# Fixed TensorE order in the experts, with weight buffers of 4 and 8 KB

## The chip, the cores and the metric

The kernel runs on one core of a Trainium2 chip, as one launch. The metric is the device time in microseconds; the kernel before was run three times. The profiler took one further execution of it, from which all rows below come. A core has five engines that each work through their own instructions in order: PE (matrix products), DVE, ACT and POOL (elementwise work and copies) and SP (which here only starts transfers). 16 DMA engines move data between the chip's memory and the core's own memory, SBUF, which has 128 partitions.

## The reference

One layer of a streaming encoder over 512 tokens of width 1024, in f32: a mixing block (pooling mixer and sparse attention), cross-attention into 256 memory tokens, and a mixture of experts. The last of these is what the change is about. A router takes the best of 4 groups and, in it, the best 2 of 8 experts for each token; each of the 32 experts has three matrices of 1 MB:

```python
h = rmsnorm(x, g)                       # (512, 1024)
for g in range(4):                      # groups of 8 experts
    a = einsum('nd,edf->nef', h, w_gate[g])     # 1024 -> 256
    b = einsum('nd,edf->nef', h, w_up[g])       # 1024 -> 256
    hid = silu(a) * b * gates[:, g, :, None]
    out += einsum('nef,efd->nd', hid, w_down[g])  # 256 -> 1024
x = x + out
```

## The kernel before

The layer before the experts works in four tiles of 128 tokens. After the cross-attention, `ffn_in(t)` (L1085 on) takes tile t of the residual x: PE transposes it, ACT and DVE copy the transposes (L1104, L1109), ACT sums the squares (L1105) and starts two transfers of the rows, to `hd`, a table in memory (L1106), and to the output `out` (L1107). Router products (L1115), `route` (L971 on: DVE finds groups and experts) and `seats` (place of a token in its expert) follow. `select` makes a 0/1 matrix from tokens to seats.

Each expert has 64 seats. The experts go in 16 pairs, and the two of a pair use the two column halves of PE. For pair i the kernel does this, all in f32:

- `slot_rows` and `slot_factors` (L1040, L1048), for two pairs at a time: PE multiplies the 0/1 matrix by small columns (L1034), which gives the row index of each seat (`idx`) and its two factors (`gc`).
- `fetch` (L1059): POOL starts a gather of the 128 rows from `hd` by `idx`, into one of three buffers. `buffer` (L1016) sets such a buffer to zero on POOL when it is first used.
- `turn_rows` (L1072): 8 transposes of 128x128 on PE into one tile of PSUM (`sc`), scaled by DVE to `xt`.
- `experts` (L1203): 32 matmuls of gate, 32 of up; each takes 64 seats by 128 rows of the weight's 1024 (chunk c of 8, for both experts k in turn). SiLU on ACT (L1208), product on DVE (L1213).
- `rest`: two transposes of the hidden values (L1219), 16 matmuls of down (L1230), copies of y by ACT and DVE (L1232, L1233), and a scatter by POOL (L1235) that adds the rows of y to `out` by `idx`.

What sets the order: the program is written once, and a scheduler (the Tile framework) then orders each engine's instructions and puts in the waits. Buffers for everything large are kept by `Slots`: 42 buffers of 4 KB per partition, and 8 more when an earlier pool is closed. `Stream` loads weights ahead through them, in the order of their use: whenever a buffer is put back, `pump` starts the next load as long as a reserve of free buffers stays (the numbers r1 to r7). The buffer that a load gets is fixed when the program is built, first freed, first used, and the load waits at run time for the last reader of that buffer. A matrix of an expert is loaded in two halves of 512 KB, 128 partitions by 4 KB; `do_load` (L249) starts them all on SP. The 96 matrices make 192 loads.

Transfers that SP and ACT start share eight completion semaphores in turn, so each waits for the one eight places before it.

Of the kernel before, what the change touches and what calls it, by code (L numbers as in the profile page):

```python
# [36 lines left out]
NSLOT = 42  # L37
NSLOT2 = 8
NG_BUF = 3
# [9 lines left out]
           t0=44, tp=1.75, a0=128, ap=1.6, d1=1, d2=2, r1=10, r2=10, r3=4, r4=11, r5=3, raw=3, raw2=4, mm=4,  # L49
# [11 lines left out]
class Slots:  # L61


    def __init__(self, pool, n):
        self.pools, self.free, self.n, self.where = {}, [], 0, {}
        self.on_put = lambda: None
        self.more(pool, n)

    def more(self, pool, n):
        self.pools.update({s: pool for s in range(len(self.pools), len(self.pools) + n)})  # L70
        self.free += list(self.pools)[-n:]

    def get(self, shape, dt):
        s = self.free.pop(0)
        self.n += 1
        t = self.pools[s].tile(shape, dt, tag=f"s{s}", name=f"s{s}_{self.n}")
        self.where[id(t)] = (s, t)
        return t

    def take_out(self):  # L80
        return self.free.pop(0)

    def again(self, s, shape, dt):
        self.n += 1
        return self.pools[s].tile(shape, dt, tag=f"s{s}", name=f"s{s}_{self.n}")

    def put(self, *tiles):
        for t in tiles:
            self.free.append(self.where.pop(id(t))[0])
        self.on_put()  # L90


class Stream:
# [28 lines left out]
    def pump(self, need=None):  # L122
# [3 lines left out]
        while True:  # L126
# [4 lines left out]
            elif (self.n_load < len(self.items) and len(self.S.free) >= 1 + keep  # L131
# [60 lines left out]
def kernel(ctx, tc, A, out, dbg=None):  # L192
# [10 lines left out]
    S = Slots(slot_pool, NSLOT)  # L203
# [42 lines left out]

    def do_load(src, shape):
        raw = S.get(shape, F32)
        sp.dma_start(raw, src)  # L249
        return raw  # L250

    def do_split(raw, gain, eng):
        shape = list(raw.shape)
        hi, lo = S.get(shape, F32R), S.get(shape, F32R)
# [233 lines left out]
    def evac_k(t, ps):  # L488
# [10 lines left out]
        if t % 2 == 0:  # L499
            kT[t // 2] = [S.get([P, 2, 4, P], F32R) for _ in range(2)]  # L500
# [96 lines left out]
    def load_bands():  # L597
        pw["b"] = [S.get([P, 1024], F32R) for _ in range(2)]
# [140 lines left out]
    def memory():  # L739
# [9 lines left out]
        kmT.extend(S.get([P, MH, MT], F32R) for _ in range(2))  # L749
# [77 lines left out]
    def transposed(t):  # L827

        hl = [S.get([P, NC, P], F32R) for _ in range(2)]
# [124 lines left out]
    row = keep.tile([P, NT, 2], F32R, name="row")  # L954
    row_f = keep.tile([P, NT, 2], F32, name="row_f")
    inf = keep.tile([P, NT, NPR, 4], F32R, name="inf")
# [3 lines left out]
    pool.tensor_copy(row, row_f)  # L960
# [69 lines left out]
    def per_slot(sel, i, cols_of, n):  # L1030

        pi = tr_tile([P, 512])
        for t in range(NT):
            pe.matmul(pi[:, :n], sel[:, t, cols(i)], cols_of(t), start=(t == 0), stop=(t == NT - 1))  # L1034
        return pi[:, :n]

    def slot_rows(j):
        for i in range(2):
            idx = fin.tile([P, 1], I32, tag="idx", name="idx", bufs=6)
            dve.tensor_scalar(idx, per_slot(sels[j], i, lambda t: row[:, t], 2)[:, 0:1], float(OOB), None, op0=OP.add)  # L1040
            tabs_[2 * j + i] = [idx, None]

    def slot_factors(j):
        sel = sels.pop(j)
        for i in range(2):
            gc = fin.tile([P, 2], F32, tag="gc", name="gc", bufs=6)
            pi = per_slot(sel, i, lambda t: inf[:, t, 2 * j + i], 4)
            dve.tensor_reduce(gc, pi.rearrange("p (a b) -> p a b", b=2), axis=AX.X, op=OP.add)  # L1048
            tabs_[2 * j + i][1] = gc

    def fetch(i):

        if i >= NPR:
            return
        if i % 2 == 0 and i not in tabs_:
# [302 lines left out]
```

## Time and profile before

| | us |
|---|---|
| median of 3 runs | 618.62 |
| lowest, highest | 615.48, 623.16 |
| the profiled execution | 623.07 |
| its span | 621.2 |
| PE busy in the span | 558.6 (90%) |
| DVE, ACT, POOL busy | 312.9, 191.7, 115.1 |

The span runs from the first to the last instruction of the profiled execution; its time is the device's, and has some 2 us around the span. The mean clock granted to PE in it is 0.944 of full speed. The first 340 us are the layer up to the router, in which weights are loaded ahead; the experts' matmuls run from 365 to 606 us. In the rows, a number of a stretch is from the start of the span. "out<-in" gives the tile written and the tile read by the program's names, "xN" the count, and a bracket the idle time of the engine ahead of the row and what ended it.

### The profile page before, as it was taken

The page shows a single profiled execution, that of the slowest core. Times are in us where ns is not written, and L with a number is a line of the kernel's source. Part 1 is how long each engine was busy: PE and PEld are TensorE (multiplying, and loading weights), DVE is VectorE, ACT ScalarE, POOL GpSimd, SP SyncE. Part 2 cuts the span into 40 slices and gives each one's busy share as a digit, 9 for nine tenths or more (in the row PEclk, how much of TensorE's full clock was granted, in tenths as well). Part 3 has the DMA queues.
Part 4 walks back from the last instruction along what each step waited for, and adds up shares of the span by engine and source line. Part 5 has one row for each costly group of instructions (what it writes and reads, how often), then busy time and mean ns, then how long its engine had stood idle before and what let it go on. Part 6 is the DMA issues. An engine that isn't in the chain of part 4 may idle for free.

```text
span 621.2 us, 9049 instructions
## 1 busy us (share of the span) xinstructions
PE 558.6 (90%) x3408; PEld 395.8 (64%) x3408; DVE 312.9 (50%) x752; ACT 191.7 (31%) x366; POOL 115.1 (19%) x94
## 2 busy tenths in 40 slices
PE   8997989999979999999989589979898979899880
PEld 4776766887767777788878466555555555555430
DVE  4598999998996656544435723222222222022000
ACT  5573534424555567764432110101010100001000
POOL 0323331201363000030001211121212121211111
PEclk9998999999989999999989759979897989899996
DMA  8963021326661201129999849999999999999962
GB/s 291 379 207 103 1 69 68 121 82 190 217 216 41 79 0 35 32 79 324 336 338 365 309 135 344 396 397 391 399 382 386 357 383 360 390 355 372 339 222 32
DMA packets 52833, 147.86 MB, mean 238 GB/s; under 512 B 10288, under 2 KB 11056, under 8 KB 52784
## 3 DMA queue, kind: packets, MB, share of 16 engines
q1 hardware_dynamic: 47024, 134.62, 59.6%
q0 software_dynamic: 4608, 8.40, 5.6%
q10 hardware_dynamic: 1152, 4.19, 1.7%
q8 instruction: 29, 0.48, 0.3%
q14 instruction: 20, 0.16, 0.1%
HBM read 142.99 MB, written 12.58 MB: 250 GB/s over the span
## 4 chain that ended last, share of the span: by engine, by line
PE 65%; DMA 15%; DVE 9%; issue 4%; ACT 3%; POOL 2%; SPq 0%; POOLq 0%; DVEq 0%; ACTq 0%
PE mm L1203 15%; PE mm L342 9%; PE mm L343 9%; PE mm L344 8%; PE mm L1230 8%; DMA out_dram<-s,idx 6%; DMA s<-in_w_up_dram 2%; PE sc L352 2%; PE sc L1072 2%; DMA s<-in_w_down_dram 2%; DMA s<-in_w_in_dram 2%; PE tr L1034 2%; PE tr L919 1%; PE tr L698 1%; PE tr L711 1%
## 5 line engine op out<-in xcount | busy, mean ns | idle before, releaser
L1203 PE MATMUL mm<-s,s 128*64 128x256 f32 x1024 | 135.9, 409 | 5.5 <-ACT sg L1208 3.5
L342 PE MATMUL mm<-s,s 128*128 128x512 f32 (+1 forms) x320 | 132.5, 417 | 0.9 <-ACT s L257 0.7
L343 PE MATMUL mm<-s,s 128*128 128x512 f32 (+1 forms) x320 | 127.6, 399 | 1.2 <-DVE s L259 0.8
L344 PE MATMUL mm<-s,s 128*128 128x512 f32 (+1 forms) x320 | 127.6, 399 | 0.0
L1203 PEld LDWEIGHTS mm<-s,s 128*64 128x64 f32 x1024 | 80.1, 147 | 54.7 <-issue 15.3
L342 PEld LDWEIGHTS mm<-s,s 128*128 128x128 f32 (+1 forms) x320 | 60.6, 190 | 16.7 <-issue 2.8
L343 PEld LDWEIGHTS mm<-s,s 128*128 128x128 f32 (+1 forms) x320 | 60.7, 190 | 14.8 <-DVE s L259 1.7
L344 PEld LDWEIGHTS mm<-s,s 128*128 128x128 f32 (+1 forms) x320 | 60.7, 190 | 13.9 <-issue 0.9
L1230 PE MATMUL mm<-s,hT 128*64 128x512 f32 x256 | 64.7, 604 | 1.2 <-issue 1.2
L1232 ACT COPY s<-mm 128x512 f32<-128x512 f32 x16 | 9.4, 585 | 153.1 <-PE mm L1230 153.1
L259 POOL TENSOR_TENSOR s<-s,s 128x1024 fp32r<-128x1024 f32 x17 | 41.2, 2428 | 74.0 <-ACT s L257 72.7
L1235 POOL DMA_INDIRECT out_dram<-s,idx x16 | 25.4, 1584 | 147.0 <-DVE hT L1221 49.4
L257 ACT CAST s<-s 128x1024 fp32r<-128x1024 f32 (+1 forms) x42 | 42.2, 1018 | 30.2 <-DMA s<-in_xattn_wkv_dram 9.4
L1213 DVE SCALAR_TENSOR_TENSOR sg<-mm,gc,sg 128x256 f32<-128x256 f32 x16 | 7.7, 484 | 66.6 <-PE mm L1203 66.6
L1230 PEld LDWEIGHTS mm<-s,hT 128*64 128x64 f32 x256 | 22.0, 141 | 29.1 <-issue 23.5
L259 DVE TENSOR_TENSOR s<-s,s 128x1024 fp32r<-128x1024 f32 (+1 forms) x25 | 33.2, 1331 | 7.0 <-ACT s L257 5.7
L1233 DVE COPY s<-mm 128x512 f32<-128x512 f32 x16 | 11.1, 692 | 48.3 <-PE mm L1230 48.3
L1208 ACT ACTIVATE sg<-mm,gc 128x256 f32<-128x256 f32 x16 | 7.6, 474 | 77.7 <-PE tr L1219 40.3
L1059 POOL DMA_INDIRECT s<-hd,idx x16 | 16.6, 1038 | 72.9 <-DVE idx L1040 66.4
L587 DVE MAX8 m<-s 128x8 f32<-128x256 f32 (+2 forms) x48 | 26.6, 554 | 0.3
L1073 DVE TENSOR_TENSOR s<-sc,gcol 128x1024 f32<-128x1024 f32 x16 | 19.6, 1222 | 13.1 <-PE sc L1072 13.1
L588 DVE MATCH_REPLACE8 s<-m,s 128x256 f32<-128x256 f32 (+2 forms) x48 | 26.0, 541 | 0.0
(209 smaller groups left out, 697.7 us busy)
## 6 DMA issues: line engine op xcount, KB each, us to landing
s<-in_w_up_dram SPq DMA_DIRECT2D x64, 512.0 KB, 11.4
s<-in_w_gate_dram SPq DMA_DIRECT2D x64, 512.0 KB, 11.6
s<-in_w_down_dram SPq DMA_DIRECT2D x64, 512.0 KB, 11.4
s<-in_w_in_dram SPq DMA_DIRECT2D x20, 512.0 KB, 7.4
s<-in_x_dram SPq DMA_DIRECT2D x8, 512.0 KB, 7.8
s<-in_xattn_wkv_dram SPq DMA_DIRECT2D x8, 512.0 KB, 4.8
s<-in_w_out_dram SPq DMA_DIRECT2D x8, 512.0 KB, 4.3
s<-in_xattn_wq_dram SPq DMA_DIRECT2D x4, 512.0 KB, 4.2
```

The lines of the kernel that those rows point to most:

```text
L257: act.copy(hi, raw)
L259: eng.tensor_tensor(lo[:, c], raw[:, c], f32(hi[:, c]), op=OP.subtract)
L342: pe.matmul(ps, ah, bh, start=start, stop=False)
L343: pe.matmul(ps, ah, bl, start=False, stop=False)
L344: pe.matmul(ps, al, bh, start=False, stop=stop)
L587: dve.max(m8, a)
L588: dve.match_replace(a, m8, a, TAKEN)
L1059: pool.indirect_dma_start(out=buffer("g", i % NG_BUF, [P, D]), out_offset=None, in_=hd, in_offset=bass.IndirectOffsetOnAxis(ap=tabs_[i][0] ...
L1073: dve.tensor_tensor(xt, pt, gcol[:, :, None].to_broadcast([P, NC, P]), op=OP.mult)
L1203: pe.matmul(pg[ks, u], xt[:, c, ks], W[k, c // 4][:, c % 4], start=(c == 0), stop=(c == NC - 1), skip_group_check=True)
L1230: pe.matmul(py[m][ks], hT[:, c, ks], W[k, c][:, m * 512:(m + 1) * 512], start=(c == 0), stop=(c == 1), skip_group_check=True)
L1235: pool.indirect_dma_start(out=out, out_offset=bass.IndirectOffsetOnAxis(ap=idx, axis=0), in_=y, in_offset=None, bounds_check=T - 1, oob_is ...
```

## The change

It has five parts.

1. **Buffers.** `Slots` keeps 18 buffers of 4 KB and 12 of 8 KB, and 4 more of 8 KB later, 50 units of 4 KB as before. `get_whole` gives an expert matrix one 8 KB buffer if one is free and was freed no later than two of 4 KB; the load is then one DMA of 1 MB with rows of 8 KB. Otherwise two buffers of 4 KB are used and two loads, as before. The 192 loads become 74 whole ones and 44 halves. Pairs of tiles that belong together elsewhere (hi and lo parts of a split weight) share an 8 KB buffer (`get_pair`).
2. **PE's order.** Matmuls and transposes of the experts are kept in the order in which the program is written: gate(i), up(i), down(i-1), the transposes of the rows of i+1, in every second pair the tables of later pairs, the transposes of the hidden values of i. In the last pair down(14) comes first, and the last matrices are loaded in that order too.
3. **Tables.** Row index and factors come from one product of 128x6 columns in place of 128x2 and 128x4; `idx` and `gc` have 8 buffers in place of 6.
4. **Rows.** Transposed rows go to two tiles of PSUM, four each, which DVE scales one after the other. Gathers use two buffers in place of three; these are set to zero by ACT instead of POOL, after `ffn_in(3)`.
5. **The start.** The last tile's rows go to `out` from SP instead of ACT, behind a transfer of 4 bytes ("mark") that waits for the index table of pair 0; SP's loads are from there on kept in program order.

```diff
@@ class Slots
+    def get_pair(self, shape, dt):
+        if not self.free2:
+            return [self.get(shape, dt) for _ in range(2)]
+        s = self.free2.pop(0)
+        t = self.tile(s, [P, 2, *shape[1:]], dt)
+        self.left[s] = 2
+        return [self.hold(t[:, i], s, t) for i in range(2)]
+
+    def get_whole(self, shape):
+        two, ones = self.free2[:1], self.free1[:2] if len(self.free1) >= 2 + self.owed else []
+        when = lambda v: max(self.freed[s] for s in v)
+        half = [shape[0], shape[1] // 2, *shape[2:]]
+        if two and (len(ones) < 2 or when(two) <= when(ones)):
+            s = self.free2.pop(0)
+            t = self.tile(s, shape, F32)
+            self.left[s] = 2
+            h = shape[1] // 2
+            return [(slice(None), t)], [self.hold(t[:, i * h:(i + 1) * h], s, t) for i in range(2)]
+        h = shape[1] // 2
+        parts = [self.get(half, F32) for _ in range(2)]
+        return [(slice(i * h, (i + 1) * h), p) for i, p in enumerate(parts)], parts
...
@@ do_load
-        raw = S.get(shape, F32)
-        sp.dma_start(raw, src)
+        if int(np.prod(shape[1:])) > 1024:
+            loads, parts = S.get_whole(shape)
+            for c, t in loads:
+                ins = sp.dma_start(t, src[:, c])
+                if held_back:
+                    tc.keep_in_program_order(ins)
+            return parts
...
@@ buffer
-            pool.memset(kept[name, n], 0.0)
+            act.activation(kept[name, n], cst[:, :1].to_broadcast(shape), AF.Copy, scale=0.0)
...
@@ turn_rows
-        pt = sc_tile().rearrange("p a (c s) -> p (a c) s", s=P)
-        for c in range(NC):
-            pe.transpose(pt[:, c], gk[:, c], ident)
-        dve.tensor_tensor(xt, pt, gcol[:, :, None].to_broadcast([P, NC, P]), op=OP.mult)
+        for k, pt in enumerate((sc_tile()[:, 0].rearrange("p (c s) -> p c s", s=P), mm_tile([P, 4, P]))):
+            ks = slice(4 * k, 4 * k + 4)
+            for c in range(4):
+                po.transpose(pt[:, c], gk[:, 4 * k + c], ident)
+            dve.tensor_tensor(xt[:, ks], pt, gcol[:, ks, None].to_broadcast([P, 4, P]), op=OP.mult)
...
@@ behind ffn_in(3)
+    mark = keep.tile([1, 1], I32, name="mark")
+    held_back.append(sp.dma_start(mark, tabs_[1]["idx"][0:1]))
+    tc.keep_in_program_order(sp.dma_start(out[cols(3)], x[3]))
+    S.put(x.pop(3))
...
@@ moe_pass
-        turn_rows(0)
-        before = iter(())
-        for i in range(NPR):
-            before = experts(n, i, before)
+        turn_rows(0)
+        hT = None
+        for i in range(NPR):
+            if i == NPR - 1:
+                down(n, i - 1, hT)
+            hid = gate_up(n, i)
+            if 0 < i < NPR - 1:
+                down(n, i - 1, hT)
+            if i == 0:
+                tables(1, 0, 6)
+                fetch(2)
+            turn_rows(i + 1)
+            if i % 2 and i + 3 < NPR:
+                tables((i + 3) // 2, 0, 6)
+            fetch(i + 3)
+            hT = turn_hid(hid)
...
```

In the ordered program, three places are of interest. The first is PE at the start of the experts, ahead of the first gate. Before (row index products 128x2, factor products 128x4, transposes of the rows into sc; s_280 is the 0/1 matrix of pairs 2 and 3):

```order
L1034 MATMUL tr<-row,s_280_3427 128x2 x4
L1072 MATMUL sc<-cst,s_268_3297 128x128 x3
L1034 MATMUL tr<-row,s_280_3427 128x2 x2
L1072 MATMUL sc<-cst,s_268_3297 128x128 x2
L1034 MATMUL tr<-row,s_280_3427 128x2 x2
L1072 MATMUL sc<-cst,s_268_3297 128x128 x3
L1034 MATMUL tr<-inf,s_280_3427 128x4 x8
L1203 MATMUL mm<-s_223_2952,s_281_3463 64x256
```

And after the change (s_196 is the 0/1 matrix of pairs 0 and 1, s_199 the gathered rows):

```order
L1119 MATMUL tr<-inf,s_196_3210 128x4 x8
L1122 MATMUL sc<-cst,s_199_3258 128x128 x4
L1122 MATMUL mm<-cst,s_199_3258 128x128 x4
L1119 MATMUL mm<-s_165_2893,s_206_3341 64x256
L1119 MATMUL mm<-s_167_2897,s_206_3341 64x256
```

The tables of pairs 2 and 3, which stood among the transposes and behind them, now stand behind the 64 matmuls of gate and up of pair 0, as one 128x6 group.

The second place is ACT at the last tile of `ffn_in`. Before (L1105 the sum of squares, L1104 the copy, s_150 and s_151 the tiles x of t=2 and t=3):

```order
L1106 DMA hd<-s_150_1569 128x1024
L1104 COPY s_263_3214<-tr 128x512
L1107 DMA out_dram<-s_150_1569 128x1024
L1104 COPY s_272_3307<-tr 128x512
L1105 ACTIVATE s_273_3308,s_2923<-s_151_1583 128x1024
L1106 DMA hd<-s_151_1583 128x1024
L1107 DMA out_dram<-s_151_1583 128x1024
```

And after the change (L1193, L1194, L1195 and L1197 are the same four lines, L1101 is the setting to zero):

```order
L1195 DMA hd<-s_111_1530 128x1024
L1193 COPY s_189_3123<-tr 128x512
L1197 DMA out_dram<-s_111_1530 128x1024
L1101 ACTIVATE s_199_3258<-cst 128x1024
L1193 COPY s_197_3214<-tr 128x512
L1194 ACTIVATE s_198_3215,s_2864<-s_112_1544 128x1024
L1195 DMA hd<-s_112_1544 128x1024
```

One setting to zero stands ahead of the copy, the sum and the transfer of t=3; its buffer was that of x of t=2, so that it waits for both transfers of that tile. The transfer of t=3 to `out` has left the engine.

The third place is SP around the mark. After the change (128x2048 is a whole matrix, 128x1024 a half):

```order
L328 DMA s_194_3206<-in_w_gate_dram 128x2048
L328 DMA s_195_3208<-in_w_up_dram 128x2048
L1263 DMA mark<-idx 1x1
L1264 DMA out_dram<-s_112_1544 128x1024
L328 DMA s_202_3316<-in_w_up_dram 128x2048
L328 DMA s_203_3318<-in_w_down_dram 128x1024
L328 DMA s_204_3319<-in_w_down_dram 128x1024
L328 DMA s_207_3371<-in_w_down_dram 128x2048
L328 DMA s_208_3373<-in_w_gate_dram 128x1024
L328 DMA s_209_3374<-in_w_gate_dram 128x1024
```

Before, the loads stood there one behind the other, each of them 128x1024, with no transfer of another kind among them. The load into s_204 waits for the transfer to `out`, whose source had that buffer, and the one into s_207 for the end of the first gate. Behind the mark stand 58 whole loads and 34 halves.

## Rows read from the trace of the kernel before

**Rows 1.** The page's slices: GB/s moved in 40 equal slices of the span
```profile
GB/s 291 379 207 103 1 69 68 121 82 190 217 216 41 79 0 35 32 79 324 336 338 365 309 135 344 396 397 391 399 382 386 357 383 360 390 355 372 339 222 32
```
**Rows 2.** Windows of 20 us: span, busy per engine, PE clock, DMA share, GB/s
```profile
360.00:380.00 20.00, 19.04 (x127) 13.36 (x128) 4.82 (x11) 0.47 (x1) 1.99 (x2) 0.73 0.59 190
380.00:400.00 20.00, 20.00 (x155) 12.63 (x156) 6.75 (x15) 1.53 (x3) 3.59 (x3) 1.00 1.01 378
```
**Rows 3.** Chain of waits, 330 to 400 us: start us, us, what
```profile
344.80 1.70 DVE s L981
...
354.18 6.74 DMA s<-hd,idx
...
363.62 1.50 PE tr L1034 x8
365.12 6.46 PE mm L1203 x32
...
380.09 0.88 PE sc L1072 x8
```
**Rows 4.** Chain of waits, 540 to 622 us
```profile
539.90 3.67 PE mm L1203 x32
...
552.52 3.67 PE mm L1203 x32
...
566.98 12.46 DMA s<-in_w_down_dram
```
**Rows 5.** DMA, 371 to 604 us: packets, MB, share of 16 engines; median us to landing
```profile
q1 hardware_dynamic: 21516, 78.31, 87.3%
q0 software_dynamic: 3744, 6.84, 11.7%
...
s<-in_w_gate_dram SPq DMA_DIRECT2D x48, 512.0 KB, 12.0
```
**Rows 6.** DMA, 585 to 590 us, where rows of 4 KB move
```profile
DMA packets 565, 2.06 MB, mean 411 GB/s; under 512 B 63, under 2 KB 63, under 8 KB 565
...
q1 hardware_dynamic: 565, 2.06, 102.7%
```
**Rows 7.** DMA, 36 to 40 us, where rows of 2 KB move
```profile
DMA packets 822, 1.59 MB, mean 396 GB/s; under 512 B 48, under 2 KB 48, under 8 KB 822
...
q1 hardware_dynamic: 822, 1.59, 104.6%
```
**Rows 8.** DMA, 295 to 296 us: one packet of the instruction queue
```profile
q14 instruction: 1, 0.01, 1.9%
```
**Rows 9.** Waits of SP, 372 to 604 us: total us, times, longest
```profile
SPq L249 <- DMA s<-in_w_gate_dram: 51.6, 44, 3.8
...
SPq L249 <- PE mm L1203: 13.4, 22, 3.5
```
**Rows 10.** Groups by line, PE, 380 to 600 us: busy, mean ns, idle before
```profile
L1034 PE MATMUL tr<-inf,s 128*128 128x4 f32 x48 | 7.9, 273 | 12.9 <-DVE idx L1040 11.7 <-DVE hT L1221 1.2
```
**Rows 11.** Timeline of DVE, 350 to 351 us: start us, us, what
```profile
350.33 0.17 DVE L981 TENSOR_SCALAR s<-s 128x4 f32<-128x4 f32 x1
```
**Rows 12.** Timeline of POOL, 340 to 372 us
```profile
344.63 1.84 POOL L1016 MEMSET s<- 128x1024 f32 x2 [5.72 <-PE tr L1102]
```
**Rows 13.** Line 1107, 336 to 360 us: the last two transfers to out
```profile
L1107 ACTq DMA_DIRECT2D out_dram<-s x2: 339/392/445, 337.3 to 345.2; - x2
...
DMA to landing us min/median/max: 7.2/8.4/9.6
```
**Rows 14.** Timeline of ACT, 334 to 346 us
```profile
344.53 0.59 ACT L1104 COPY s<-tr 128x512 f32<-128x512 f32 x1 [6.64 <-PE tr L1102]
```
**Rows 15.** Timeline of SP, 330 to 380 us
```profile
352.03 17.53 SPq L249 DMA_DIRECT2D s<-in_w_down_dram  x4
```
**Rows 16.** Timeline of DVE, 603 to 612 us
```profile
605.79 0.69 DVE L1233 COPY s<-mm 128x512 f32<-128x512 f32 x1 [3.98 <-PE mm L1230]
```
**Rows 17.** Timeline of POOL, 590 to 622 us
```profile
608.85 1.56 POOL L1235 DMA_INDIRECT out_dram<-s,idx  x1 [5.05 <-DMA out_dram<-s,idx]
```

More of the change, by code (lines that the diff above doesn't have):

```diff
@@ L61, with __init__ @@
 class Slots:
-    def __init__(self, pool, n):
-        self.pools, self.free, self.n, self.where = {}, [], 0, {}
-        self.on_put = lambda: None
[L67 to L71, printed above, removed]
-    def get(self, shape, dt):
[L74 to L78, printed above, removed]
+    def __init__(self, pool, ones, twos):
+        self.pool_of, self.free1, self.free2, self.spare = {}, [], [], []
+        self.where, self.left, self.n, self.clock = {}, {}, 0, 0
+        self.freed = {}
+        self.owed = N_OWN
+        self.on_put = lambda: None
+        self.more(pool, ones, twos)
@@ new lines, in more, with free, tile @@
+    def more(self, pool, ones, twos):
+        for k, (free, n) in enumerate(((self.free1, ones), (self.free2, twos))):
+            for _ in range(n):
+                s = len(self.pool_of)
+                self.pool_of[s] = pool
+                self.freed[s] = 0
+                free.append(s)
+    @property
+    def free(self):
+        return range(len(self.free1) + 2 * len(self.free2) + len(self.spare))
+    def tile(self, s, shape, dt):
+        self.n += 1
+        return self.pool_of[s].tile(shape, dt, tag=f"s{s}", name=f"s{s}_{self.n}")
@@ new lines, in hold @@
+    def hold(self, v, s, of):
+        self.where[id(v)] = (s, of, v)
+        return v
+    def get(self, shape, dt):
+        if self.free1:
+            s = self.free1.pop(0)
+            return self.hold(self.tile(s, shape, dt), s, None)
+        n = int(np.prod(shape[1:]))
+        names = "abc"[:len(shape) - 1]
+        at = next((p for p in self.spare if p[2] == dt), None)
+        if at is None:
+            s = self.free2.pop(0)
+            t = self.tile(s, [P, 2, 1024], dt)
+            self.left[s] = 1
+            half = 0
+            self.spare.append((s, t, dt))
+        else:
+            self.spare.remove(at)
+            s, t, _ = at
+            self.left[s] += 1
+            half = 1
+        v = t[:, half, :n]
+        if len(names) > 1:
+            v = v.rearrange(f"p ({' '.join(names)}) -> p {' '.join(names)}", **dict(zip(names, shape[1:])))
+        return self.hold(v, s, t)
@@ L80, in take_out, with room @@
+    def room(self, shape, keep):
+        if int(np.prod(shape[1:])) <= 1024:
+            return len(self.free) >= 1 + keep
+        return len(self.free) >= 2 + keep and (bool(self.free2) or len(self.free1) >= 2 + self.owed)
     def take_out(self):
[L81 to L85, printed above, removed]
+        self.owed = max(0, self.owed - 1)
+        return self.free1.pop(0)
@@ L87, in put @@
+    again = tile
     def put(self, *tiles):
+        self.clock += 1
         for t in tiles:
-            self.free.append(self.where.pop(id(t))[0])
+            s, of, _ = self.where.pop(id(t))
+            if of is None:
+                self.free1.append(s)
+            else:
+                self.left[s] -= 1
+                if self.left[s]:
+                    continue
+                self.spare = [p for p in self.spare if p[0] != s]
+                self.free2.append(s)
+            self.freed[s] = self.clock
@@ L1198, in experts @@
         for u, name in enumerate(("gate", "up")):
-            W = {(k, c): ST.take((n, i, name, k, c)) for k in range(2) for c in range(2)}
+            W, held = expert(n, i, name)
             for c in range(NC):
```

160 lines of the change are left out of this document (83 added, 77 removed).

## The prediction

> **What bounds the kernel now.** I read the slices of the page first. From 340 us on, apart from one dip, they move 340 to 399 GB/s: the expert matrices are streamed [rows 1]. The 20 us windows show who is busy there: from 380 to 400 us the DMA engines are full (1.01) and PE has 20.00 us of 20, while in the 20 us before DMA stands at 0.59 [rows 2]. Two resources are nearly full, so the next view is the chain of waits. With the experts' first matmul at 365.12 us it goes over to PE [rows 3]; a weight enters it only at 566.98 us [rows 4]. From there on it is loads of weights, and then the last down and scatter. Read together: PE starts with the 42 half-matrices loaded ahead, uses them up faster than DMA refills, and is caught near 567 us. So the end is set by **when DMA starts again after the buffers are full, how fast it moves the 148 loads that are left, and what comes after the last one**. PE's own order in between costs nothing unless it delays a buffer.
>
> How full DMA is: between 371 and 604 us SP issues 148 loads of 512 KB (48 of gate, 48 of up, 52 of down); the loads take 87.3% of the 16 engines, gathers and scatters 11.7% [rows 5]. What a 4 KB packet costs at best is seen at 585 to 590 us: 102.7% x 16 x 5 us / 502 (565 packets less 63 small ones) = 163.7 ns [rows 6]. Then 148 x 128 x 163.7 ns / 16 = 193.8 us, and 11.7% x 233 = 27.3 us, together 221. **12 us of the 233 are slow packets and gaps.**
>
> **The change part by part**, against the profiled execution, 623.07 us (0.7% above the median 618.62; the sum is scaled by 0.993).
>
> *8 KB rows.* Behind the mark SP issues 58 whole loads and 34 halves, where there were 150 halves. 58 x 128 pairs of 4 KB packets become one 8 KB packet each. No weight in the trace has such rows. A 2 KB packet costs 104.6% x 16 x 4 us / 774 = 86.5 ns [rows 7] and a 4 KB one 163.7: 77.2 per 2 KB, and 9.3 ns fixed. By that line 8 KB costs 318 ns and each merge saves 9.3: 58 x 128 x 9.3 / 16 = **-4.3 us**. The ends: nothing, if 8 KB costs two 4 KB packets (327 ns); and -10.9 by the one 8 KB packet that can be priced alone, an instruction fetch of 1.9% x 16 x 1 us = 304 ns [rows 8]. I take the line, since the weights' own rows make it. A loss is not excluded, but no row prices one.
>
> The Trainium skill (DMA: Bandwidth & Descriptors, Why small descriptors are slow) puts the fixed cost of a packet at about 3 cycles and 32 bytes of metadata and finds joining descriptors worthwhile only up to 256 B. At that page's 850 MHz I estimate 5 ns, and by it the saving would be 2 us.
>
> *Fewer, larger DMAs in flight.* SP spends 51.6 us in 44 waits on gate loads, which are waits for the DMA eight places back, and much the same on up and down; 13.4 us go to PE [rows 9]. Eight places can now hold whole matrices, up to twice the bytes, so a gap is covered better. Of the 12 us I credit **-1.5**; the ends are 0 and -12.
>
> *Buffers freed later.* Gate and up run through chunks 0 to 7, so the first halves of both experts came free half-way; a whole buffer comes free at the end. Half a gate is 1.8 us of 3.67 [rows 4], and 3.2 of the first one's 6.46 [rows 3]. As the end of a gate frees four halves, some 5 us of DMA work, the loss is paid at the restart and hardly again: **+2**, with 0 and +23 (rival A) as ends.
>
> *PE's order and the tables.* One 128x6 group replaces a 128x2 and a 128x4 group, and PE no longer meets an index table whose buffer an earlier scatter still holds: 11.7 us of idle before L1034 from 380 to 600 us [rows 10]. All of it lies before 567 us, where PE is ahead: a pair takes PE 12.6 us (539.90 to 552.52, [rows 4]) and its 12 loads, at 399 GB/s [rows 1], take DMA 15.8. So **0**; if that cover were gone, -11.7.
>
> *Start of the experts.* The gather lands at 360.92 (354.18 + 6.74); the gate starts at 365.12. Between them stand 8 transposes of the rows mixed with the next pair's index tables, and then 1.50 us of its factor tables [rows 3]. These tables move behind up(0). What remains is 8 transposes, 0.88 us when nothing is between them [rows 3], and the scaling of a half, in all some 1.5: **-2.7**. The router's chain: a DVE scalar step stands on it with 1.70 us [rows 3] where the same step alone takes 0.17 [rows 11], because POOL writes its memset of 1.84 us beside it [rows 12]. POOL's memset goes: -1.6. But ACT now does it ahead of the copy of t=3, in a buffer that x[2] had, whose write to out is issued at 337.3 and lands 7.2 us later at the earliest, at 344.5 [rows 13]. A pass of ACT over twice the width of the 0.59 us copy, some 1.1 us, so comes ahead of the copy that started at 344.53 [rows 14]: +1.1. Net **-0.5**. The gather, 6.74 us, now has out(3) and the held loads beside it in place of what was queued there: **+1** (-1 to +4). Together -2.2, with -4 and +4 as ends.
>
> What the mark holds back: SP issues nothing until the index of pair 0 is there, about 353 us; at 352.03 SP had a stretch of 17.53 us for four loads [rows 15] because buffers were full, so 0. A half load behind it waits for out(3) to land, with the whole loads queued behind that; by 7.2 to 9.6 us [rows 13] it is through by 363, before the first gate can free anything.
>
> *Tail.* The last y was there at 606.48 (605.79 + 0.69, [rows 16]) and its scatter began at 608.85, behind the previous one [rows 17]. Now down(14) precedes gate(15), and that scatter is long done: -2.4. Against it, the last matrices arrive whole and PE can't begin on their halves, half of a down: +1.9. Net **-0.5**.
>
> *Everything before the experts* is reshuffled by the scheduler, as hi and lo share a buffer: **0**, plus or minus 4.
>
> Sum: -4.3 - 1.5 + 2 - 2.2 - 0.5 = -6.5, so 616.6 on the profiled execution and **612** on the median. A measurement of this kernel can tell about 2%, 12.4 us: faster is below 606.2, slower above 631.0.
>
> **Rivals.**
> *A, slower: whole buffers starve DMA.* SP's queue is in order, and every load waits for the buffer that the plan gave it. If the late halves cost DMA each time until PE's lead is gone, not once, the price is 3.2 us for the first gate and 1.8 for each of the other 11 matrices of four pairs, 23 us in place of 2: 637.6, on the median **633**. It decides where PE's release, not the place eight back, is what SP waits for last. For it: 13.4 us of such waits are there already. Against it: that is a quarter of the 51.6 us that waits on gate loads alone take [rows 9]. 0.10.
>
> *B, 8 KB rows move no faster*, because a packet is cut or the memory is the limit: the change then does only its smaller parts. -6.5 + 4.3 = -2.2, 620.9, on the median **616**. For it: 411 GB/s is the most that any stretch shows [rows 6]. Against it: the line through 2 and 4 KB, and the 304 ns. 0.20.
>
> The Trainium skill (DMA: Bandwidth & Descriptors, Specifications) gives a core about 358 GB/s of HBM; by that rule larger rows would bring nothing, as in B. The trace disagrees, with 411 GB/s over 5 us and 399 over a slice.
>
> *C, the lost 12 us come back.* If the gaps and slow packets come from the number of DMAs and packets, most go: a further -10.5, sum -17, 606.1, on the median **602**. For it: slices of 396 to 399 GB/s stand beside some of 339 to 366 with the same work [rows 1]. Against it: the scatters and gathers, which mix in, stay. 0.25.
>
> The forecast, 605 to 620 about 612, has 0.45.
>
> **Numbers.** Low 600 takes in most of C; high 623 takes in B and the forecast with the start at its bad end; outside are A and the edges, 0.15 to 0.2. Faster: most of C and a tenth of the forecast, 0.27. Slower: A, 0.10. Same: 0.63.
>
> **What would show it.** In the changed profile: 8 KB packets near 318 ns (327 or more: B); the first expert matmul within 2 us of the gather's landing; SP waiting on PE for under 30 us in all (over 40: A); time lost beyond the floor near 10 us (under 3: C); no last scatter waiting for the one before. I would be wrong altogether if PE instead of weights stood on the chain up to the end, or if the part before 340 us moved by more than 4 us.

## The result, and the profile after

The changed kernel takes 625.2 us (median of 20 runs, 620.53 to 627.17), the kernel before 618.46 (20 runs, 615.48 to 625.01). The ratio is 1.0085, with a 95% interval of 1.0062 to 1.0107: some 5 us slower, where I had forecast 6.5 faster. Some executions fall into a slower state of the chip; a ratio, here and below, compares executions outside it alone, so that it can differ a little from the quotient of two medians. The profiled execution took 627.06 us, with a span of 624.9.

The first view is the page's slices, as in [rows 1]. Where the weights stream without a break, from the 26th slice to the 35th, they move at 380 to 407 GB/s, before at 357 to 399:

```profile
GB/s 299 395 180 134 1 35 101 123 63 128 237 145 132 68 10 1 68 35 201 313 294 407 332 199 316 396 405 404 407 403 391 398 380 402 392 338 417 389 96 27
```

So the loads do move faster. In the windows that answer to [rows 2], the columns are the span, the busy time per engine, the PE clock, the DMA share and GB/s. PE is busy for 14.70 us at a clock of 0.63, where it was 19.04 at 0.73:

```profile
360.00:380.00 20.00, 14.70 (x88) 10.56 (x89) 7.16 (x35) 2.07 (x3) 2.27 (x2) 0.63 0.56 199
380.00:400.00 20.00, 18.02 (x144) 11.30 (x142) 8.06 (x25) 1.06 (x2) 4.81 (x4) 1.00 1.00 393
```

The chain of waits from 350 to 385 us tells why. It answers to [rows 3]: start, length, what. The router's step is down to 0.18 us from 1.70, since POOL no longer writes beside it. But the gather starts at 363.56, not 354.18, and the first gate at 370.64, not 365.12:

```profile
359.68 0.18 DVE s L1066
...
363.56 5.07 DMA s<-hd,idx
...
370.64 5.62 PE mm L1119 x32
```

From the gather's landing (368.63) to the gate it is 2.0 us, where the forecast had left 1.5. All of the loss lies ahead of the gather: the first transposes of the router's input, for t=0, began at 327.20 us, where they began at 320.13 before.

A late first gate becomes a late end because the loads now set the pace much earlier. In the changed profile the chain of waits goes over to a load at 407.39 us and stays with loads up to 586 us; in the kernel before, a weight entered it only at 566.98 ([rows 4]):

```profile
407.39 16.62 DMA s<-in_w_gate_dram
```

The loads themselves, from 376 to 606 us, answer to [rows 5]. There are 13,245 packets in place of 21,516, and a load of 1 MB lands after 19 us:

```profile
q1 hardware_dynamic: 13245, 78.63, 84.2%
q0 software_dynamic: 4096, 7.52, 13.1%
...
s<-in_w_gate_dram SPq DMA_DIRECT2D x19, 1024.0 KB, 19.2
```

Between 391.5 and 396.5 us nearly all packets are of 8 KB. One takes 101.2% x 16 x 5 us / 251 = 322.5 ns, against 2 x 163.7 for two halves; my line said 318. The shares also hold the small packets and what a packet loses in traffic. Packet by packet, in the trace's records from 376 to 606 us, the median is 309 ns for 8 KB and 159 ns for 4 KB, so that one merge saves 9 ns, as the line had it:

```profile
DMA packets 283, 2.06 MB, mean 411 GB/s; under 512 B 32, under 2 KB 32, under 8 KB 32
...
q1 hardware_dynamic: 283, 2.06, 101.2%
```

SP's waits of the same stretch answer to [rows 9]. Waits on PE have grown from 13.4 to 40.0 us, the bound that I had set for rival A, neither under 30 nor over 40:

```profile
SPq L328 <- DMA s<-in_w_gate_dram: 44.6, 21, 3.9
SPq L328 <- PE mm L1119: 40.0, 15, 8.0
```

At the end, the last scatter starts at 612.62, and it waits for the last y, not for the scatter before it ([rows 16, 17]); the copy of y starts at 611.17:

```profile
602.31 1.55 POOL L1332 DMA_INDIRECT out_dram<-s,idx  x1 [7.77 <-DMA out_dram<-s,idx]
612.62 1.55 POOL L1332 DMA_INDIRECT out_dram<-s,idx  x1 [8.75 <-DVEq L1382]
```

### The profile page after: what moved, and what is told of

It is laid out like the page before. It is cut to its first block, busy times and chain, and to the rows that moved or that the text cites. A ratio compares the mean times of both kernels' runs of the same rounds, so it can differ in the third digit from the quotient of the medians.

```text
span 624.9 us, 8827 instructions
## 1 busy us (share of the span) xinstructions
PE 554.9 (89%) x3352; PEld 384.6 (62%) x3352; DVE 314.0 (50%) x768; ACT 194.2 (31%) x368; POOL 116.0 (19%) x91
## 3 DMA queue, kind: packets, MB, share of 16 engines
q10 hardware_dynamic: 1008, 3.67, 1.5%
## 5 line engine op out<-in xcount | busy, mean ns | idle before, releaser
L1119 PE MATMUL mm<-s,s 128*64 128x256 f32 x1024 | 122.7, 387 | 13.9 <-ACT sg L1306 9.4
L430 PE MATMUL mm<-s,s 128*128 128x512 f32 (+1 forms) x320 | 128.7, 402 | 0.0
L1119 PEld LDWEIGHTS mm<-s,s 128*64 128x64 f32 x1024 | 72.6, 139 | 60.5 <-ACT sg L1306 16.7
L1119 PE MATMUL mm<-s,hT 128*64 128x512 f32 x256 | 67.1, 639 | 10.3 <-DMA s<-in_w_down_dram 8.8
L428 PEld LDWEIGHTS mm<-s,s 128*128 128x128 f32 (+1 forms) x320 | 61.5, 192 | 20.5 <-issue 4.6
L429 PEld LDWEIGHTS mm<-s,s 128*128 128x128 f32 (+1 forms) x320 | 61.5, 192 | 15.4 <-issue 3.2
L430 PEld LDWEIGHTS mm<-s,s 128*128 128x128 f32 (+1 forms) x320 | 61.2, 191 | 14.1 <-issue 1.1
L345 POOL TENSOR_TENSOR s<-s,s 128x1024 fp32r<-128x1024 f32 x17 | 42.1, 2485 | 87.4 <-ACT s L343 66.2
L1119 PEld LDWEIGHTS mm<-s,hT 128*64 128x64 f32 x256 | 19.9, 145 | 47.9 <-issue 29.6
L345 DVE TENSOR_TENSOR s<-s,s 128x1024 fp32r<-128x1024 f32 (+1 forms) x25 | 31.0, 1245 | 5.5 <-ACT s L343 5.3
L769 ACT ACTIVATE p<-p,rsm,fq 128x128 f32<-128x128 f32 (+3 forms) x32 | 20.6, 646 | 4.3 <-DVE rsm L767 4.2
```

Source lines behind the costliest of these rows:

```text
L345: eng.tensor_tensor(lo[:, c], raw[:, c], f32(hi[:, c]), op=OP.subtract)
L428: pe.matmul(ps, ah, bh, start=start, stop=False)
L429: pe.matmul(ps, ah, bl, start=False, stop=False)
L430: pe.matmul(ps, al, bh, start=False, stop=stop)
L769: act.activation(ph, ph, AF.Exp, bias=m[:, h, 1:2], scale=f[:, h:h + 1], accum_out=m[:, h, 2:3])
L1119: return tc.keep_in_program_order(pe.matmul(*a, **k))
```

## The experiments

Each was timed against the kernel before on the same chip. A ratio is to that kernel.

**Buffers or start?** Two theories stood for the 7 us by which the experts were late: mixed buffers of 4 and 8 KB reorder the part ahead (T), or the new start and order cost them (U). Four kernels tell them apart.

`e1`, the change with buffers of 4 KB alone:

```diff
-N_ONE, N_TWO, N_TWO_MORE, N_OWN = 18, 12, 4, 7
+N_ONE, N_TWO, N_TWO_MORE, N_OWN = 42, 0, 4, 7
...
-    S.more(..., 0, N_TWO_MORE)
+    S.more(..., 2 * N_TWO_MORE, 0)
```

> The changed kernel with 50 buffers of 4 KB and no 8 KB one; PE's fixed order, tables, rows and the new start stay. Theory T (the mixed buffers reorder the part before the experts, which costs the 7 us by which ffn_in of tile 0 began later, 327.2 instead of 320.1): that part is again as before, PE's first transposes of ffn_in at 320 +- 1, first gate at 363 to 364, time 616 to 619 (the kernel before, less some 2 at the start; no gain of 8 KB rows). Theory U (the new start and fixed order are the loss): 623 to 627, as the changed kernel, and ffn_in at 327.

619.68 us, ratio 0.999 (0.9956 to 1.0025). The first transposes are at 316.76 us, even earlier than T's 320. T holds, and no effect of everything else in the change together is seen.

`e2`, the kernel before with the new buffers alone:

```diff
-NSLOT = 42
-NSLOT2 = 8
+N_ONE, N_TWO, N_TWO_MORE, N_OWN = 18, 12, 4, 8
...
+            loads, parts = S.get_whole(shape)
...
```

> The kernel before with the buffers of the change alone: 18 of 4 KB, 12 and 4 of 8 KB, 75 whole loads and 42 halves; PE's order, tables, gathers, start and last pair are those of before. T: ffn_in at 327 +- 1, 8 KB rows give 2 to 8 us back, time 619 to 624, slower than or equal to before. U: ffn_in at 320, time 611 to 616.

640.76 us, ratio 1.034 (1.0295 to 1.0384); the first transposes at 322.25. T by its sign, but not at its 327, and the loss is three times as large: the experts lose too. From the first SiLU to the last scatter they take 251.2 us (375.29 to 626.49), before 237.2 (371.65 to 608.85).

`e3`, 8 KB buffers only among the late ones:

```diff
-N_ONE, N_TWO, N_TWO_MORE, N_OWN = 18, 12, 4, 7
+N_ONE, N_TWO, N_TWO_MORE, N_OWN = 42, 0, 4, 7
```

> The changed kernel with 42 buffers of 4 KB from the start and 8 KB ones only among the four that come when the attention is over: 20 whole loads, 152 halves. T: ffn_in at 320, first gate at 363 to 364, about a quarter of the gain of 8 KB rows, time 614 to 618. U: 622 to 626.

620.07 us, 1.0009 (0.998 to 1.0038), the transposes at 316.60. The early part is as T says. A gain of 1 to 2 us by the 20 whole loads can't be told from none at this interval.

`e4`, PE's order left to the scheduler:

```diff
-            return tc.keep_in_program_order(pe.matmul(*a, **k))
+            return pe.matmul(*a, **k)
```

> The changed kernel with PE's matmuls of the experts left to the scheduler's order; all else stays. T: ffn_in still at 327; PE's order costs or gives at most 2 us, time 623 to 627. U, as far as the fixed order is the loss (PE waits in order for late down matrices): 617 to 621.

647.61 us, 1.0447 (1.0401 to 1.0493). Neither theory has this, and the transposes, at 323.84, are not at T's 327 either. The waits of PE from 376 to 640 us (total, times, longest) name the place:

```profile
PE sc L1122 <- DMA s<-hd,idx: 27.4, 5, 7.3
```

PE stands at the transposes of gathered rows. On its timeline the scheduler put them where the gather that refills the only other buffer had just been started (508.94 on POOL):

```profile
517.46 1.09 PE L1122 MATMUL sc<-cst,s 128*128 128x128 f32 x4 [5.00 <-DMA s<-hd,idx]
```

**Two gather buffers, or 8 KB packets?** `e10` is `e4` with `NG_BUF = 3` (and `N_OWN` 8); `e11` is `e1` with the scheduler's order.

> The changed kernel with PE's experts in the scheduler's order (as in the run with free order, 647.6 us) and three gather buffers in place of two. Theory G (the free order puts the transposes of the next rows right behind the gather that refills the only other buffer, and PE waits 31.5 us in 6 gathers): with a third buffer these waits go to below 8 us, time 620 to 630. Theory P (8 KB packets slow gathers and scatters, whatever the buffers): waits stay over 20 us, 638 to 648.

627.86 us, 1.0141 (1.0092 to 1.0189); the waits for gathers are 1.9 us.

> Buffers of 4 KB only (as in the run with 619.7 us), but PE's experts in the scheduler's order, two gather buffers. G: two buffers in free order cost PE the gathers here too, 630 to 642. P: with 4 KB packets the gathers are in time, 617 to 622.

630.9 us, 1.0211 (1.0155 to 1.0267); 24.6 us of waits for gathers in 6. Two buffers in a free order are the cause of these waits, whatever the packets. Much the same waits cost 22 us with mixed buffers (`e4` against the change) and 14 with 4 KB ones (`e11` against `e1`); why the price differs was not followed up. In the fixed order two are enough, as the third buffer in `e16` shows:

```diff
-N_ONE, N_TWO, N_TWO_MORE, N_OWN = 42, 0, 4, 7
+N_ONE, N_TWO, N_TWO_MORE, N_OWN = 42, 0, 4, 8
-NG_BUF = 2
+NG_BUF = 3
```

> The 4 KB run with three gather buffers in place of two; PE's order stays fixed. In that order the gather has 12 us for its 9, so a third buffer brings nothing in time and takes one 4 KB unit from the weights: 619 to 622. If gathers are late for PE in the fixed order too: 614 to 618.

620.72 us, 0.9997 (0.9969 to 1.0025), as `e1`.

**What are the 8 KB rows worth?** `e5` keeps every buffer and the order on PE and DVE, and issues a whole load as two (`...` stands for the rest of a line).

```diff
-            return [(slice(None), t)], [self.hold(...
+            return [(slice(i * h, (i + 1) * h), t[:, i * h:(i + 1) * h]) for i in range(2)], [self.hold(...
```

> The changed kernel with the same buffers and the same order on PE and DVE, but each whole load issued as two DMAs of 512 KB with rows of 4 KB into the halves of its buffer. Theory R (8 KB rows shorten the loads by the 4 us that 318 against 2 x 163.7 ns make): last load 3 to 5 us later against the first gate, time 627 to 630. Theory N (an engine that lags behind the others sets when loads land, and rows do nothing for it): 624 to 626.5. Theory H (8 KB packets and 8 MB in flight delay gathers and scatters, 11.0 us to landing against 7.5 before, and that costs PE): 619 to 623.

629.61 us, 1.0165 (1.0128 to 1.0202). Against it the change is 0.8% faster, 4.9 us (2.2 to 7.6 by the two intervals): R. But `e5` also puts half as many bytes into the eight places, so the 4.9 us hold the rows and the larger DMAs in flight together. Against `e1`'s 0.999 the mixed buffers cost 1.75%, 10.8 us (7.7 to 13.9).

`e6` was meant to keep the rows and halve the bytes in flight:

```diff
-                ins = sp.dma_start(t, src[:, c])
+                for r in (slice(0, 64), slice(64, 128)) if len(loads) == 1 else (slice(None),):
+                    ins = sp.dma_start(t[r], src[r, c])
```

> The changed kernel with each whole load issued as two DMAs of 64 partitions by 8 KB: the rows stay 8 KB, the eight places hold 4 MB again and not 8. R: rows are what counts, 624 to 626.5, loads landing in 12 us and not 19. N: as R. H, as far as the bytes in flight are what delays gathers: gathers land in 8 to 9 us, 620 to 624. If the deep queue hid gaps (my term of 1.5 us): 626 to 632.

798.47 us, 1.2792 (1.2724 to 1.2861). The question stays open, since loads of 64 partitions are slow in themselves: from 400 to 700 us of the profiled execution (801.12 us) the engines are full and move 227 GB/s, and by the packet records the median 8 KB packet takes 575 ns, where it takes 309 in the change. Fewer bytes in flight are not the reason, as `e5` has them too and moves 367 GB/s.

```profile
DMA packets 14522, 68.10 MB, mean 227 GB/s; under 512 B 3749, under 2 KB 3749, under 8 KB 8689
...
q1 hardware_dynamic: 11184, 61.90, 91.6%
```

The Trainium skill (DMA: Bandwidth & Descriptors, Rules for kernel authors) advises one transfer over 128 partitions, as two halves would merely come one after the other. Here they cost more than that: the same bytes took two thirds longer, by 227 against 375 GB/s.

**How many 8 KB buffers, and is it luck?** `e7` (38, 2, 4 later: 28 whole loads), `e8` (34, 4, 4: 37), `e13` (22, 10, 4: 65) change the counts (the edit shown first is that of `e13`), `e12` one reserve:

```diff
-N_ONE, N_TWO, N_TWO_MORE, N_OWN = 18, 12, 4, 7
+N_ONE, N_TWO, N_TWO_MORE, N_OWN = 22, 10, 4, 7
...
-r2=10
+r2=8
```

> The changed kernel with 38 buffers of 4 KB and 2 of 8 KB from the start, 4 of 8 KB later: 28 whole loads and 136 halves. PE's order ahead of the experts is nearly that of before. Theory T (mixed buffers reorder the early part): ffn_in as with 4 KB only (317 to 320), time 617 to 621. If any 8 KB buffer in the early part costs the 7 us: 624 to 627.

> The changed kernel with 34 buffers of 4 KB, 4 of 8 KB and 4 later: 37 whole loads, 118 halves. PE's order ahead of the experts differs from before from its 191st matmul on, as that of the change does from its 180th. T, if a reordered early part is what costs: ffn_in at 322 to 328, time 621 to 627. If the size of the reordering matters (1622 of 1717 matmuls in place against 1619 in the change): the same as the change, 625.

> The changed kernel with one number of the stream's reserve altered (r2 8, not 10), which moves loads of the early part; 74 whole loads as in the change, 1635 of 1717 matmuls ahead of the experts in the order of before against 1619. If the early part's order is what costs, and the loss is a matter of where a few stalls fall: ffn_in anywhere from 317 to 327 and the time moves with it, 615 to 626. If the mixed buffers cost as such: 624 to 627.

> The changed kernel with 22 buffers of 4 KB and 10 of 8 KB, 4 later: 65 whole loads and 62 halves, 1645 of 1717 matmuls in the order of before. Same question: 615 to 626 by where ffn_in begins, or 624 to 628 if mixed buffers cost as such.

The ratios are 1.0018 (0.9985 to 1.0051), 1.018 (1.0148 to 1.0212), 1.0103 (1.0061 to 1.0145) and 1.014 (1.0097 to 1.0183). The table has, from each profile, the start of the first transposes of the router's input and of the first SiLU (us):

| run | 8 KB buffers early | transposes | first SiLU | ratio |
|---|---|---|---|---|
| before | 0 | 320.13 | 371.65 | 1 |
| e1 | 0 | 316.76 | 362.74 | 0.999 |
| e3 | 0 | 316.60 | 362.58 | 1.0009 |
| e7 | 2 | 320.50 | 364.23 | 1.0018 |
| e8 | 4 | 323.01 | 372.30 | 1.018 |
| e13 | 10 | 328.97 | 375.86 | 1.014 |
| e12 | 12 | 323.27 | 372.58 | 1.0103 |
| e5 | 12 | 326.30 | 373.56 | 1.0165 |
| the change | 12 | 327.20 | 376.29 | 1.0085 |

All but the first row have the new start. Not one of the five with four or more early 8 KB buffers has its first SiLU before 372 us; with none or two it is at 363 to 364. `e12` and `e13` came out where mixed buffers cost as such, so the loss isn't the luck of one order; `e8`'s 1.018 lies above both readings that were on record. Among the five neither column orders the ratios: each row is one execution, and executions of one kernel differ by some us.

**The other terms, one at a time on `e1`.** `e14` undoes the start (five edits; the core):

```diff
-    mark = keep.tile([1, 1], I32, name="mark")
-    held_back.append(sp.dma_start(mark, tabs_[1]["idx"][0:1]))
-    tc.keep_in_program_order(sp.dma_start(out[cols(3)], x[3]))
...
-            act.activation(kept[name, n], cst[:, :1].to_broadcast(shape), AF.Copy, scale=0.0)
+            pool.memset(kept[name, n], 0.0)
```

> The 4 KB run with the start of before: rows of t=3 to out from ACT, gather buffers set to zero on POOL ahead of ffn_in(3), no mark, SP's loads not held. Theory S (the new start saves what I put down, 0 to 2 us, the rest of the earlier start comes from the tables' place): first SiLU within 2 us of the 4 KB run's 362.7, time 618 to 622. If the mark and ACT's zeros are what made the start earlier: first SiLU at 366 to 371, 621 to 625. If they cost: below 618.

617.57 us, 0.9936 (0.9905 to 0.9967): 0.6% under the kernel before, clear of the interval though below the 2% that counts as faster, and 0.54% under `e1`. By the two ratios the new start costs 3.3 us (0.5 to 6.2).

`e17` undoes the zeros on ACT alone (the last two lines above, in the new place):

> The 4 KB run with the gather buffers set to zero by POOL, in the new place behind ffn_in(3). On ACT the first zeros wait for x of t=2 to reach out and hold up the copy of t=3 by 2 us; on POOL they are out of that way: 616.5 to 619.5, unless POOL's zeros slow a DVE step of the router again (1.84 us beside a step of 1.70 in the kernel before): 619 to 621.

617.79 us, 0.9954 (0.9925 to 0.9983). That is 2.2 us under `e1`, but the two intervals overlap, and `e1`'s own profile gives the zeros less: there they wait for two matmuls and not for x of t=2, and the copy of t=3 begins at 341.60, 0.45 us after its transposes ended (340.51 + 0.64). `e15` undoes the last pair's order (`sorted(...)` in `add_experts`, the first `down` in `moe_pass`):

> The 4 KB run with the last pair as in the other pairs: gate and up of 15, then down 14, then down 15, and the loads in that order. If the new tail is worth the 2.4 us of the scatter's wait: 621 to 623. If PE's backlog at the end makes it worth nothing: 618.5 to 621. If it costs (down 14 waits, gate 15 behind it): 615 to 618.

618.88 us, 0.9991 (0.996 to 1.0022), as `e1`: nothing to see within 3 us either way. The profile has the scatter's wait back. The last y is there at 601.07 (600.38 + 0.69), and its scatter begins 3.0 us later:

```profile
604.10 1.55 POOL L1332 DMA_INDIRECT out_dram<-s,idx  x1 [5.74 <-DMA out_dram<-s,idx]
```

In `e1` the scatter begins 0.7 us after the last y (601.47, 602.21). But counted from the first SiLU that y comes at 238.7 us, in `e15` at 236.3, and the scatters begin at 239.5 and 239.4: the new tail gains the wait and loses as much in PE's work.

`e18` is the changed kernel with the start of `e14`; `e19` is `e14` with the four late buffers of 8 KB.

> The changed kernel with the start of before (rows of t=3 to out from ACT, zeros on POOL ahead of ffn_in(3), no mark, SP's loads not held); buffers, 8 KB rows, PE's order, tables and last pair as in the change. If the terms add: 1.0085 - 0.0054 = 1.003 of before, 620 to 623, still not faster. If the new start was put in because mixed buffers need it (held loads keep SP's order): 625 to 632.

621.55 us, 1.0041 (1.0017 to 1.0066): the terms add. Against it the new start costs the change 2.7 us (0.7 to 4.8), and the profiles place that: from the first transposes to the first SiLU the change takes 49.1 us and `e18` 45.9 (323.94 to 369.86).

> The 4 KB run with the old start (0.9936), and the four late buffers of 8 KB: 20 whole loads, 152 halves. By a quarter of the rows' gain 1 us faster, 0.990 to 0.994; with the new start these buffers gave nothing (1.0009 against 0.999), by which it would be 0.994 to 0.997.

620.36 us, 1.0015 (0.9986 to 1.0045): a loss of 0.8% against `e14`, outside both readings on record. `e14` has the lowest ratio, with `e17` beside it within the intervals; both lie under the kernel before and the change.

## Why the prediction was wrong

From kernel to kernel, all but the new start and the mixed buffers gives -4.0 us (`e14` against the kernel before), the new start +3.3 (`e1` against `e14`), mixed buffers +10.8 (`e5` against `e1`), whole loads in them -4.9 (the change against `e5`). These are steps of one path, so they come to the measured +5.2 of 618.5 by construction; each has an interval of 2 to 3 us to either side. The -4.0 also hold two numbers of the stream's reserve, which the list of the change leaves out: r4 goes from 11 to 10 and r5 from 3 to 6, in the change and in every kernel here but `e2`. They were not tried alone.

*The step that failed* is the term for everything before the experts, "reshuffled by the scheduler", put at 0, plus or minus 4. I had treated the early part as a shuffle without a sign. It has one, and my own sign of being wrong altogether came true: the part before 340 us moved by 7 us. One profile of one kernel would be weak evidence, but in all ten profiles with four or more early 8 KB buffers the first transposes begin at 321.61 to 328.97 us, and in all ten with none or two at 315.80 to 320.50.

Most of the loss sits in one stretch, the attention, where PE computes scores in groups of 12 products (L438). From the first such group to the third, the change takes 25.8 us (from 192.99) and `e1` 17.8 (from 193.70):

```profile
204.56 0.98 PE L438 MATMUL sc<-s,s 64*128 64x256 f32 x12
218.81 0.90 PE L438 MATMUL sc<-s,s 64*128 64x256 f32 x12
```
```profile
202.80 0.97 PE L438 MATMUL sc<-s,s 64*128 64x256 f32 x12
211.50 0.90 PE L438 MATMUL sc<-s,s 64*128 64x256 f32 x12
```

The same stretch takes 23.1 to 25.8 us in the ten profiles with four or more early 8 KB buffers, and 17.5 to 18.9 in the ten others. What happens in it is seen on SP. SP's queue is in order, so a load that waits holds up the next ones. On its timeline of the change, the last load of the output projection is issued at 194.01 us, behind loads of another matrix that had to wait:

```profile
166.89 19.59 SPq L333 DMA_DIRECT2D s<-in_w_out_dram  x7
188.65 5.31 SPq L333 DMA_DIRECT2D s<-in_xattn_wq_dram  x2
194.01 0.46 SPq L333 DMA_DIRECT2D s<-in_w_out_dram  x1
```

In `e1` all eight are in one row that starts earlier:

```profile
159.65 21.01 SPq L333 DMA_DIRECT2D s<-in_w_out_dram  x8
```

From 140 to 215 us, SP's loads of the change wait for the steps on POOL and DVE that split an earlier load in two (L345); those of `e1` wait mostly for matmuls (L430), the readers of buffers from further back:

```profile
SPq L333 <- POOL s L345: 24.4, 8, 4.0
SPq L333 <- DVE s L345: 24.3, 7, 10.6
```
```profile
SPq L333 <- PE mm L430: 46.6, 8, 15.9
```

So with mixed buffers a load gets a buffer that another load has only just left. That the 18 buffers of 4 KB, and an 8 KB buffer that comes free only with its second half, are why, is read from the code of `Slots`; it was not tried by itself.

What follows from the late load, in the change, is read across ACT, DVE and PE. ACT waits for it to cast it. Behind the cast stands ACT's part (L349) of another matrix, DVE waits for that with its own part (L350), the softmax steps (L766) stand behind L350 on DVE, and PE waits for the probabilities:

```profile
198.97 1.05 ACT L343 CAST s<-s 128x1024 fp32r<-128x1024 f32 x1 [3.98 <-DMA s<-in_w_out_dram]
199.92 1.33 ACT L349 ACTIVATE s<-s,vecs 128x512 fp32r<-128x512 f32 x2
```
```profile
200.67 2.37 DVE L350 SCALAR_TENSOR_TENSOR s<-s,vecs,s 128x512 fp32r<-128x512 f32 x1 [3.15 <-ACT s L349]
202.97 0.41 DVE L766 CUSTOM_DVE_ANT_0 p<-sc,s 128x256 f32<-128x256 f32 x1
```
```profile
208.39 1.97 PE L784 MATMUL tr<-cst,p 128*128 128x128 f32 x8 [2.85 <-DVE p L776]
```

The pause costs twice. In windows of 4 us of the change, PE works 1.54 of 4 us and in the next window is granted a clock of 0.50, the lower of its two levels (1.2 of 2.4 GHz):

```profile
204.00:208.00 4.00, 1.54 (x15) 0.97 (x13) 2.05 (x9) 2.45 (x8) 0.00 (x0) 0.92 0.64 189
208.00:212.00 4.00, 3.61 (x21) 3.03 (x23) 3.17 (x14) 1.93 (x5) 0.00 (x0) 0.50 0.16 62
```

In `e1` both windows are full at a clock of 1.00:

```profile
204.00:208.00 4.00, 4.00 (x33) 3.18 (x32) 3.98 (x14) 2.90 (x8) 0.00 (x0) 1.00 0.00 2
208.00:212.00 4.00, 4.00 (x24) 3.13 (x24) 2.71 (x7) 1.21 (x5) 0.69 (x4) 1.00 0.39 80
```

This chain was followed in the change. The late single load of the output projection stands in SP's timeline of all nine kernels with ten or twelve early 8 KB buffers, at 190 to 199 us; `e8` lost as much in the stretch with its eight loads out earlier, and its chain was not followed. Rival A had this mechanism, "every load waits for the buffer that the plan gave it", and I had looked for it only in the experts.

*8 KB rows, -4.3, and fewer gaps, -1.5*: -4.9 (2.2 to 7.6) for the two together, which `e5` doesn't part. The mechanism of the rows is borne out by the packets, 9 ns saved in a merge for the line's 9.3. The Trainium skill's small fixed cost (DMA: Bandwidth & Descriptors, Why small descriptors are slow), by which I had estimated 5 ns, is below these 9 ns; the 2 us that it makes lie at the edge of the interval. Rival B falls. So does rival C: by 322.5 and 163.7 ns the 58 whole and 34 half loads take 194 us of an average engine, gathers and scatters 30, and of the 230 us some 6 are still lost, where C wanted under 3. What fewer and larger DMAs give by themselves is open, because `e6` failed to test the bytes in flight.

*Buffers freed later, +2*: between the first SiLU and the last scatter `e1` takes 239.5 us (362.74 to 602.21) and `e5` 243.8 (373.56 to 617.36). In these two executions that is +4.3. But `e16`, with 4 KB buffers alone, takes 243.9 too (364.74 to 608.68), so the size of this term is not shown. The 40.0 us of SP's waits on PE are of this kind; how many of them were covered is not shown either. In the two profiles the early part makes 10.8 us; they lie 14.8 us apart, 4 more than the ratios, so both numbers are rather high.

*PE's order and the tables, 0*: not contradicted. `e14` gains 4.0 us, and for what it holds I had -2.7 (the tables' new place, under the start) and -0.5 (the tail). Its profile agrees on the place: from the first transposes to the first SiLU it takes 45.6 us (315.80 to 361.41), before 51.5, and from there to the last scatter it is no faster, 239.5 for 237.2. What I had not priced is that two gather buffers need the fixed order: with them the scheduler's order costs 2.2% (`e11` against `e1`), as the waits for gathers show. In `e2`, with before's order and three buffers, PE idles 18.0 us at the index tables, for 11.7 in [rows 10]; the rest of the 14 us that its experts lose was not traced.

*The start, -2.2*: the two terms that can be read in the change came out near the forecast (2.0 us from landing to gate for 4.2, and 0.18 for 1.70), and the gather took 5.07 us for 6.74, where I had feared +1. But the 1.70 was a matter of timing more than of the engine: in `e18`, with the zeros on POOL, that step takes 0.17 too. Against the old start, the new one was forecast at -0.5 + 1 = +0.5, and the runs have 2.7 (0.7 to 4.8) and 3.3 (0.5 to 6.2); the forecast lies at the lower end of both. I had priced ACT's zeros at +1.1 and the mark at 0. On ACT's timeline of the change the zeros wait 7.71 us for x of t=2 to reach `out`, and the copy of t=3 begins at 353.71, 2 us after its transposes ended (351.02 + 0.64):

```profile
352.75 1.05 ACT L1101 ACTIVATE s<-cst 128x1024 f32<-128x1024 f32 x1 [7.71 <-DMA out_dram<-s]
352.86 0.33 ACTq L1195 DMA_DIRECT2D hd<-s  x1
353.71 0.57 ACT L1193 COPY s<-tr 128x512 f32<-128x512 f32 x1
```

So the price of that wait was too low by 1 us. The old start isn't free of it: in `e18` the copy itself waits for that transfer and begins 1.4 us after its transposes (350.02 against 348.02 + 0.63). More of the difference is the clock. Behind the longer pause of the change PE's router products run at a granted clock of 0.52, near the lower level, and PE is busy for 3.67 us; in the window of `e18` that answers to it, at 1.00, the same work takes 2.15:

```profile
354.00:358.00 4.00, 3.67 (x23) 3.67 (x24) 0.60 (x5) 1.32 (x3) 0.54 (x1) 0.52 0.85 354
```
```profile
350.00:354.00 4.00, 2.15 (x23) 2.07 (x24) 2.54 (x15) 1.63 (x3) 0.54 (x1) 1.00 1.01 425
```

And from the gather's start to the first gate the change takes 7.1 us, `e18` 6.2. What of this is due to the mark and what to the transfer to `out` from SP was not tried.

*Tail, -0.5*: within what can be told, and right in its two terms. The wait on the scatter before is gone (3.0 us in `e15`, forecast 2.4), and the last y comes 2.4 us later (forecast 1.9).

## What to carry to other kernels

A change of a buffer's size acts wherever the buffer is used, not only where the large transfer is: before pricing it, look at which loads elsewhere now wait, for which reader of a buffer, and what stands behind them in the issuing engine's queue. A reordering that a scheduler makes need not be noise with a mean of zero; look in its order for the load that moved back and for the engine that has it at its head. And a piece of bookkeeping (zeros, a store) that is moved to an idle engine brings its waits with it: here ACT was idle some 70% of the time, and yet the zeros stood ahead of a copy that PE's router products waited for.

## What the hardware showed that I had not expected

The same bytes in the same 8 KB rows moved at 227 GB/s when a DMA covered 64 partitions, and at 375 when it covered 128. By the packet records single packets were slower, not the gaps longer.

The DMA engines don't end together. In the change, from 600 to 604 us, the load queue takes 7.2% of 16 engines, about one of them, while the rest have nothing left to do:

```profile
q1 hardware_dynamic: 26, 0.12, 7.2%
```

A load has landed when its slowest engine is through: the semaphore of the last load is raised sixteen times, fifteen of them by 601.26 us and the last at 607.11. For the same 78.6 MB the loads took 86.5% of 235.4 us in `e5` and 84.2% of 230 in the change, 203.6 and 193.7 us of an average engine, and only about half of these 9.9 us became time. That one engine lags is shown; what makes it lag is open.

With the old start the four late buffers of 8 KB cost 0.8% (`e19` against `e14`), with the new start nothing is seen (`e3` against `e1`). The two differences differ by no more than their intervals, so no cause is sought here.
